# Branch gates loaded into more buffers, K's second half behind the first head, an earlier table of weight sums, and A22 ahead of s4 in a hybrid RWKV / RG-LRU encoder block

## The chip, the cores and the metric

The kernel runs on one core of one Trainium2 chip. The metric is the device time of one execution in microseconds (us). The engines of the core are TensorE (PE in the profile, with its weight loads PEld), VectorE (DVE), ScalarE (ACT), GpSimd (POOL) and SyncE (SP). SP issues most of the loads, POOL and ACT some; all data moves through the core's 16 DMA engines.

## The reference, cut to what matters

One encoder block over 512 positions of width 1024, float32 throughout. Two sequence mixers, an RWKV-7 recurrence (`y_a`) and a gated linear recurrence (`y_b`), are merged by sigmoid gates; then come cross-attention into 256 memory rows with 4 heads, a gated feed-forward net of width 2816 and a last RMS norm.

```python
h = rms_norm(x, norm_mix_g)
proj = h @ w_in + b_in
y_a = rwkv7_branch(proj[..., :cb0], ...) @ w_branch_a
y_b = rglru_branch(proj[..., cb0:cb1], proj[..., cb1:cb2], ...) @ w_branch_b
merged = sigmoid(proj[..., cb2:cg1]) * y_a + sigmoid(proj[..., cg1:]) * y_b
x = x + merged @ w_mix_out
x = x + cross_attention(rms_norm(x, norm_x_g), rms_norm(mem, norm_mem_g), w_cq, w_ckv, w_co)
x = x + conv_ffn(rms_norm(x, norm_ffn_g), w_ffn_in, ffn_conv_w, ffn_conv_b, w_ffn_out)
return rms_norm(x, norm_final_g)

def cross_attention(h, m, w_q, w_kv, w_o):    # q, k, v reshaped to 4 heads of 256
    ...
    sc = einsum('bqhd,bkhd->bhqk', q, k) * 256 ** -0.5
    o = einsum('bhqk,bkhd->bqhd', softmax(sc), v)
    return o @ w_o
def conv_ffn(h, w_in, conv_w, conv_b, w_out):
    u = h @ w_in
    gate = causal_dwconv(u[..., :D_FF], conv_w, conv_b)
    return (gelu(gate) * u[..., D_FF:]) @ w_out
```

## The kernel before

A tensor of activations lies in SBUF as blocks of 128 features by 512 positions. A float32 product of one 128-block of weights with one block of activations is three matmuls (`mm3`): each factor is split into a rounded high part and the low rest, and high·high, high·low and low·high are summed in PSUM. The weights are streamed from HBM in tiles of 128x1024, eight units of 128x128 each (`stream`, tag `wr`, 4 buffers): SP loads the raw tile, ScalarE casts the high part (tag `wh`, 3 buffers), VectorE subtracts for the low part (tag `wl`, 3).

The program runs through these stages:

- the norm and the in-projection `inproj`, 38 blocks of 128 columns (`in_ps`). Blocks 22 to 37 are the branch gates: their sigmoids are stored to a DRAM tensor `dG`, since SBUF has no room for them. Blocks 14 to 17 (`px_gates`, `px_scan`) and 18 to 21 (`py_block`) belong to the second mixer; the chunks of the RWKV recurrence run between these products. `ga` and `gx` are tags of that part's tiles, with two buffers each; the tag `st` holds stores of gates and the tiles `ge`.
- w_branch_b: for each of the 8 output blocks m, a gate `gb` is loaded from `dG[8+m]`, the product lies in PSUM as `yb_ps`, and VectorE multiplies both into `mB`.
- w_branch_a: in the same way with a gate `gta` from `dG[m]`; VectorE multiplies `ya_ps` by it and adds `mB`, ScalarE casts the high part `mg` and VectorE subtracts for the low part. `mg` is what w_mix_out multiplies (`mix_ps`).
- cross-attention: K and V of the memory, computed at the program's start, are loaded from DRAM (`dK`, `dV`) in two halves each, through tiles of tag `kv`, and split into high and low parts (`K2`, `V2`). K's first half belongs to heads 0 and 1, its second to heads 2 and 3. `q_head(hd)` makes a head's q, `attend(hd, q2)` its scores (`sc_ps`), exponentials (`ex`), transposes (`prT`) and output. The loads `kv` are issued by ScalarE.
- w_co, then the feed-forward net. Its two large products are done by a scheme with seven products of half size in place of eight; some of them need sums of two quarters of the weights. POOL makes these sums by DMAs that accumulate in DRAM (`dS` for the first product, `dO` for the second).
- the output projection: the products A11, A12, s1, s2, s3, s4, A22, whose raw weights come by SP from `in_wfo` or from the sums `dOs`. They collect in PSUM tiles `X` and `YZ` (`ox_ps`, `oyz_ps`); `ffn_out` adds them into the residual `xr`, and `final` normalises and stores the output.

The order of the work on each engine is set by a scheduler at compile time, which simulates the program. POOL's DMAs for `dS` are tied to matmuls by hand: `sum_behind(ins, n)` issues the next n of them behind a product, and the table `NSUM` says how many go behind each block of the in-projection. Later products issue a fixed number each.

Of the kernel before, what the change touches and what calls it, by code (L numbers as in the profile page):

```python
# [9 lines left out]
F32 = mybir.dt.float32  # L10
F32R = mybir.dt.float32r
AF = mybir.ActivationFunctionType
ALU = mybir.AluOpType
# [4 lines left out]
P = 128  # L18
T = 512
D = 1024  # L20
# [11 lines left out]
IN_REST = [22, 23, 24, 25, 26, 27, 28, 29, 30, 31, 32, 33, 34, 35, 36, 37, 14, 15, 16, 17, 18, 19, 20, 21]  # L32
NEARLY = 3
NMID = 10
IN_ORDER = IN_RWKV + IN_REST


# [17 lines left out]
def hybrid_block_kernel(ctx: ExitStack, tc: tile.TileContext, xT_d, mT_d, pv_d, cst_d, win_d, wk_d, wv_d,  # L55
                        lup_d, gup_d, rga_d, rgx_d, wba_d, wbb_d, wmix_d, wq_d, wo_d, wfi_d, wfo_d, out_d):
    nc = tc.nc
    V, S, PE = nc.vector, nc.scalar, nc.tensor
# [15 lines left out]
    def rw_ps(name, pool=None, tag="rw", **kw):  # L74
        return (pool or prw).tile([P, T], F32, tag=tag, name=name, **kw)
# [193 lines left out]
    with tc.tile_pool(name="p0", bufs=1, reuse_waits="tile") as p0:  # L269
# [62 lines left out]
        st = stream(wv_d, "wv")  # L332
        for hf in range(2):
            pss = [(mm_ps if hf else rw_ps)(f"v_ps{hf}_{i}") for i in range(2)]
# [107 lines left out]
    MQ = KB // 2  # L442
# [46 lines left out]
    tp = tp_ctx.enter_context(tc.tile_pool(name="tp", bufs=1, reuse_waits="tile"))  # L489
# [19 lines left out]
    for i in range(2):  # L509
        with tc.issue_after(wdma[-1].ins):  # L510
# [5 lines left out]

    NSUM = {12: 1, 13: 1, 4: 1, 5: 1, 0: 1, 1: 1, 8: 1, 9: 1, 6: 2, 7: 2, 2: 2, 3: 2, 10: 2, 11: 2,
            22: 2, 23: 1, 27: 1, 28: 1, 29: 1, 31: 1, 32: 1, 33: 1, 34: 1, 35: 1, 36: 1,
            17: 3, 18: 4, 19: 4, 20: 4, 21: 4}

    def inproj(i):
        nonlocal last_in
# [160 lines left out]
    with tc.tile_pool(name="pz", bufs=1, reuse_waits="tile") as pz:  # L683
# [9 lines left out]
        for s in range(30, -1, -1):  # L693
            n = 31 - s
# [249 lines left out]
            V.tensor_tensor(yb2[:, 1, b, :], yb, yb2[:, 0, b, :].bitcast(F32), ALU.subtract)  # L944
    ub = Units(wbb_d, "wbb")
    for m in range(KB):
        gb = tp.tile([P, T], F32, tag="st", name=f"gb{m}", bufs=2)
        nc.sync.dma_start(gb, dG[8 + m])
        psb = mm_ps(f"yb_ps{m}")
        dense(psb, ub, lambda kb: (yb2[:, 0, kb, :], yb2[:, 1, kb, :]), 4)  # L950
        V.tensor_tensor(mB[:, m, :], psb, gb, ALU.mult)
# [6 lines left out]
    pm = pm_ctx.enter_context(tc.tile_pool(name="pm", bufs=2, reuse_waits="tile"))  # L958
    ua = Units(wba_d, "wba")
    for m in range(KB):  # L960
        ga = pm.tile([P, T], F32, tag="ga", name=f"gta{m}")
        nc.sync.dma_start(ga, dG[m])
        psa = mm_ps(f"ya_ps{m}")
        dense(psa, ua, lambda kb: (ya2[:, 0, kb, :], ya2[:, 1, kb, :]), 4)
        V.tensor_tensor(ga, psa, ga, ALU.mult)
        V.tensor_tensor(ga, ga, mB[:, m, :], ALU.add)
        S.copy(mg2[:, 0, m, :], ga)
        V.tensor_tensor(mg2[:, 1, m, :], ga, mg2[:, 0, m, :].bitcast(F32), ALU.subtract)
# [46 lines left out]
    pk = pk_ctx.enter_context(tc.tile_pool(name="pk", bufs=1, reuse_waits="tile"))  # L1015
    K2 = pk.tile([P, 2, KB, NMEM], F32R, name="K2")
    V2 = pk.tile([P, 2, 2, D], F32R, name="V2")
    for i, what in ((0, "K"), (0, "V"), (1, "V"), (1, "K")):
        kv = pk.tile([P, D], F32, tag="kv", name=f"kv{what}{i}", bufs=2)
        if what == "K":  # L1020
            ks = slice(4 * i, 4 * i + 4)
            hi, lo = K2[:, 0, ks], K2[:, 1, ks]
            kv = kv.rearrange("p (m n) -> p m n", n=NMEM)
            nc.scalar.dma_start(kv, dK[ks].rearrange("m p n -> p m n"))
        else:
            hi, lo = V2[:, 0, i], V2[:, 1, i]
            nc.scalar.dma_start(kv, dV[i])
        S.copy(hi, kv)
        V.tensor_tensor(lo, kv, hi.bitcast(F32), ALU.subtract)

    uq = Units(wq_d, "wq")

    def q_head(hd, nsum=2):
        q2 = pk.tile([P, 2, 2, T], F32R, tag="q2", name=f"q2_{hd}", bufs=2)
        for i in range(2):
            ps = mm_ps(f"q_ps{hd}_{i}")
            dense(ps, uq, lambda kb: (hx[:, 0, kb, :], hx[:, 1, kb, :]), KB, nsum + i * (nsum > 0))
            S.copy(q2[:, 0, i, :], ps)
            V.tensor_tensor(q2[:, 1, i, :], ps, q2[:, 0, i, :].bitcast(F32), ALU.subtract)
        return q2  # L1040
# [35 lines left out]
    for hd in range(4):  # L1076
        attend(hd, q2)
        if hd < 3:
            q2 = q_head(hd + 1)

    pk_ctx.close()

# [5 lines left out]
    H = T // 2  # L1088
# [164 lines left out]
    def out_weights():  # L1253

        flat = []
        for n in ("A11", "A12", "s1", "s2", "s3", "s4", "A22"):
            for m, k in out_order:
                if n[0] == "A":
                    p, i = out_units(m, int(n[1]), int(n[2]))[k]
                    flat.append((p, wfo_d[p], i))  # L1260
                else:
                    flat.append(((n, m), dO["s2" if n == "s4" else n, m], k))
        for g in range(0, len(flat), 8):
            units = flat[g:g + 8]
            n = len(units) * P
            with tc.high_priority():
                raw = wp.tile([P, 1024], F32, tag="wr", name=f"wfo_r{g // 8}", bufs=4)
                k = 0
                while k < len(units):
                    key, src, i = units[k]  # L1270
                    e = k
                    while e < len(units) and units[e][0] == key and units[e][2] == i + e - k:
                        e += 1
                    nc.sync.dma_start(raw[:, k * P:e * P], src[:, i * P:(i + e - k) * P])
                    k = e
                hi = wp.tile([P, 1024], F32R, tag="wh", name=f"wfo_h{g // 8}")
                lo = wp.tile([P, 1024], F32R, tag="wl", name=f"wfo_l{g // 8}")
                S.copy(hi[:, :n], raw[:, :n])  # L1278
                V.tensor_tensor(lo[:, :n], raw[:, :n], hi[:, :n].bitcast(F32), ALU.subtract)  # L1279
            for k in range(len(units)):  # L1280
                yield hi[:, k * P:(k + 1) * P], lo[:, k * P:(k + 1) * P]
# [3 lines left out]
    def out_product(n, i, out, start, done, nsum=0):  # L1285

        for m, k in out_order:
            wh, wl = next(uf)
            g = gsets[i][k // 8][:, k % 8]
            ins = mm3(out[m], wh, wl, g[:, 0, :], g[:, 1, :], start and k == 0, k == HB - 1,  # L1290
                      skip_group_check=not start)
            if m * HB + k < nsum:
                sum_behind(ins)
            if k == HB - 1:
                done(m)
# [10 lines left out]
    YZ = [pf.tile([P, T], F32, tag="yz", name=f"oyz_ps{m}", bufs=4) for m in range(MQ)]  # L1306
    cols = (slice(0, H), slice(H, T))
    sn1, sn5 = ([pc.tile([P, T], F32, tag="sn", name=f"{n}_{i}", bufs=3) for i in range(2)] for n in ("o1", "o5"))
    sn6 = pc.tile([P, T], F32, tag="sn", name="o6_0", bufs=3)
    p1, p5 = ([t[:, c] for t in ts for c in cols] for ts in (sn1, sn5))  # L1310
    p6 = [sn6[:, c] for c in cols]
    p6 += [pc.tile([P, H], F32, tag="p5", name=f"o6_{m}", bufs=3) for m in (2, 3)]

    def ffn_out(src, snap, sign, m, ts, first=False, last=False):

        n = ts.stop - ts.start
        if snap is not None:
            t1 = pc.tile([P, T], F32, tag="s", name=f"t1_{m}_{ts.start}")
            V.tensor_tensor(t1[:, :n], src, snap, ALU.add)
            src = t1[:, :n]  # L1320
        V.tensor_tensor(xr[:, m, ts], xr[:, m, ts], src, sign)
        sq = sso[:, ts] if first else pc.tile([P, T], F32, tag="ac", name=f"t2_{m}_{ts.start}")[:, :n]
        S.activation(sq, xr[:, m, ts], AF.Square)
        S.activation(xr[:, m, ts], xr[:, m, ts], AF.Identity, scale=par("nfin", m))
        if not first and not last:
            V.tensor_tensor(sso[:, ts], sso[:, ts], sq, ALU.add)
        return sq

    def final(ts, sq, nb):
        n = ts.stop - ts.start  # L1330
        pss = rw_ps(f"rs_ps{ts.start}", pf, "yz", bufs=4)
        PE.matmul(pss[:, :n], ones, sso[:, ts], start=True, stop=False)
        PE.matmul(pss[:, :n], ones, sq, start=False, stop=True)
        rsqrt(ro[:, ts], pss[:, :n], 1.0 / D, eps[:, 0:1], load=False)
        for m in range(0, KB, nb):
            ms = slice(m, m + nb)
            V.tensor_tensor(xr[:, ms, ts], xr[:, ms, ts], ro[:, ts].unsqueeze(1).to_broadcast([P, nb, n]), ALU.mult)
            nc.sync.dma_start(out_d[:, ms, ts], xr[:, ms, ts])

    def c12(m):  # L1340
        sq = ffn_out(YZ[m][:, H:T], p6[m], ALU.add, m, cols[1], last=m == MQ - 1)
        if m == MQ - 1:
            final(cols[1], sq, 2)

    def c21(m):
        if m < MQ - 1:
            ffn_out(X[m], None, ALU.subtract, MQ + m, cols[0])
        else:
            for o in (0, P):
                ts = slice(o, o + P)  # L1350
                final(ts, ffn_out(X[m][:, ts], None, ALU.subtract, MQ + m, ts, last=True), 4)

    prepare(1, lambda ks: g2(ks, 1))
    prepare(2, lambda ks: g1(ks, 1))
# [7 lines left out]
    prepare(1, lambda ks: g2(ks, 2))  # L1362
    out_product("s1", 2, [t[:, H:T] for t in YZ], True, lambda m: S.copy(p5[m], YZ[m][:, H:T]))
    prepare(2, lambda ks: g1(ks, 2))
    out_product("s2", 0, X, False, lambda m: S.copy(p6[m], X[m]))
    for put in out_sums(("s4",)):
        tc.keep_in_program_order(put())
    for k in K4:
        ks = slice(k, min(k + 4, HB))
        V.scalar_tensor_tensor(g1(ks, 1), g1(ks, 1), -1.0, g2(ks, 1), ALU.mult, ALU.subtract)  # L1370
        split_g(0, lambda ks: g1(ks, 1), k)
    out_product("s3", 2, X, False, lambda m: ffn_out(X[m], p5[m], ALU.subtract, MQ + m, cols[1], first=m == 0))
    out_product("s4", 1, [t[:, H:T] for t in YZ], False, c12)
    out_product("A22", 0, X, False, c21)


# [75 lines left out]
```

## Time and profile before

| | |
|---|---|
| time, 3 runs | 908.43 us median (905.87 to 909.82) |
| profiled execution | 911.28 us, span 909.5 us, granted clock 0.998 |
| TensorE busy | 886.1 us (97%), 6186 matmul records |
| VectorE, ScalarE, POOL busy | 684.8, 515.8, 131.2 us |
| DMA | 201.37 MB, mean 221 GB/s |

All times of the profile are from one execution and count from the span's start. A line of the timeline reads: start in us, duration in us, engine, source line, operation, output tile and input tiles, shape, how many were put together; in brackets how long the engine was idle before it and what ended that idle time. An engine with a "q" at its end is the engine's queue at issuing a DMA. "L948" is line 948 of the kernel before; the numbers behind tile names in the lists of order below are the compiler's.

### The profile page before, as it was taken

Reading aid. Unit: us, or ns where it says so; the run is one execution under the profiler, and the core shown is the slowest. Engines: PE = TensorE matmul, PEld = TensorE weight load, DVE = VectorE, ACT = ScalarE, POOL = GpSimd, SP = SyncE. Lnnn points to the kernel's source line nnn. Section 1 sums busy time; section 2 is a strip of 40 time slices with the busy share of each in tenths; the row PEclk is TensorE's granted clock in tenths of the full one; section 3 lists DMA queues with packets and bytes.
Section 4 is the critical chain, followed back from the end, with each engine's and each line's share of the span. In section 5 each row is a group of like instructions: output and inputs, shape, how many; then the busy total and the mean of one; then the engine's idle time right before and its main releaser. Section 6 shows DMA issues by size and latency. Waiting matters only on the chain.

```text
span 909.5 us, 15907 instructions
## 1 busy us (share of the span) xinstructions
PE 886.1 (97%) x6186; PEld 769.3 (85%) x6186; DVE 684.8 (75%) x1100; ACT 515.8 (57%) x787; POOL 131.2 (14%) x161
## 2 busy tenths in 40 slices
PE   6999999999999999989989999999999999999996
PEld 6888878888877777768867778999999999999996
DVE  7884698768957686576566568889888888999674
ACT  6674676643347675134454356766655556757563
POOL 0102222021001122001012111111111111202100
PEclk9999999999999999999999999999999999999999
DMA  8879799677876289968887958899989998988963
GB/s 273 279 269 222 191 234 226 201 200 215 264 175 161 41 176 239 261 189 229 220 215 164 214 124 184 243 273 275 271 240 301 268 284 252 245 274 207 273 193 92
DMA packets 97642, 201.37 MB, mean 221 GB/s; under 512 B 19424, under 2 KB 30816, under 8 KB 97504
## 3 DMA queue, kind: packets, MB, share of 16 engines
q1 hardware_dynamic: 63584, 118.97, 40.0%
q0 software_dynamic: 25504, 67.38, 36.4%
q10 hardware_dynamic: 8480, 14.02, 4.5%
q8 instruction: 48, 0.79, 0.3%
q14 instruction: 26, 0.21, 0.1%
HBM read 188.54 MB, written 78.12 MB: 293 GB/s over the span
## 4 chain that ended last, share of the span: by engine, by line
PE 86%; DMA 7%; DVE 5%; ACT 1%; issue 1%; SPq 0%; DVEq 0%; ACTq 0%
PE in_ps L162 8%; PE in_ps L161 8%; PE in_ps L163 7%; PE fx_ps L162 5%; PE fx_ps L161 5%; PE fx_ps L163 5%; PE fyz_ps L162 3%; PE fyz_ps L163 3%; PE fyz_ps L161 3%; DMA gb<-dG 2%; PE ox_ps L163 2%; PE ox_ps L161 2%; PE ox_ps L162 2%; PE co_ps L161 2%; PE co_ps L163 2%; PE co_ps L162 2%
## 5 line engine op out<-in xcount | busy, mean ns | idle before, releaser
L127 ACT CAST wfi_h<-wfi_r 128x1024 fp32r<-128x1024 f32 x77 | 81.0, 1052 | 81.0 <-PE fyz_ps L162 28.4
L162 PE MATMUL in_ps<-hT,win_h 128*128 128x512 f32 x304 | 121.6, 402 | 0.0
L161 PE MATMUL in_ps<-hT,win_h 128*128 128x512 f32 x304 | 121.5, 401 | 0.1
L163 PE MATMUL in_ps<-hT,win_l 128*128 128x512 f32 x304 | 121.6, 401 | 0.0
L128 DVE TENSOR_TENSOR wfi_l<-wfi_r,wfi_h 128x1024 fp32r<-128x1024 f32 x77 | 94.1, 1222 | 23.0 <-ACT wfi_h L127 22.9
L427 POOL DMA_DIRECT2D dS<-in_wfi x66 | 66.5, 1028 | 267.8 <-PE in_ps L161 134.1
L116 DVE TENSOR_TENSOR win_l<-win_r,win_h 128x1024 fp32r<-128x1024 f32 x38 | 46.3, 1222 | 30.8 <-ACT win_h L115 30.1
L161 PEld LDWEIGHTS in_ps<-hT,win_h 128*128 128x128 f32 x304 | 57.0, 188 | 14.6 <-DVE pr L531 0.6
L162 PEld LDWEIGHTS in_ps<-hT,win_h 128*128 128x128 f32 x304 | 57.0, 188 | 14.5 <-issue 0.7
L163 PEld LDWEIGHTS in_ps<-hT,win_l 128*128 128x128 f32 x304 | 57.0, 188 | 14.2 <-issue 0.7
L463 POOL DMA_DIRECT2D dOs<-in_wfo x54 | 39.9, 789 | 188.4 <-PE fyz_ps L161 48.2
L115 ACT CAST win_h<-win_r 128x1024 fp32r<-128x1024 f32 x38 | 39.8, 1048 | 43.1 <-PE in_ps L162 40.4
L1279 DVE TENSOR_TENSOR wfo_l<-wfo_r,wfo_h 128x1024 fp32r<-128x1024 f32 (+1 forms) x39 | 47.1, 1209 | 16.2 <-ACT wfo_h L1278 14.6
L1278 ACT CAST wfo_h<-wfo_r 128x1024 fp32r<-128x1024 f32 (+1 forms) x39 | 40.4, 1038 | 30.2 <-DMA wfo_r<-dOs 8.0
L163 PE MATMUL ox_ps<-go,wfo_l 128*128 128x256 f32 x176 | 49.5, 281 | 1.2 <-DVE wfo_l L1279 1.2
L162 PE MATMUL fx_ps<-hr,wfi_h 128*128 128x256 f32 x176 | 49.8, 283 | 0.0
L161 PE MATMUL ox_ps<-go,wfo_h 128*128 128x256 f32 x176 | 49.8, 283 | 0.0
L163 PE MATMUL fx_ps<-hr,wfi_l 128*128 128x256 f32 x176 | 49.8, 283 | 0.0
L162 PE MATMUL fx_ps<-hq,wfi_h 128*128 128x256 f32 x176 | 49.4, 281 | 0.0
L162 PE MATMUL fyz_ps<-hq,wfi_h 128*128 128x256 f32 x176 | 49.4, 281 | 0.0
L161 PE MATMUL fx_ps<-hr,wfi_h 128*128 128x256 f32 x176 | 49.4, 280 | 0.0
L162 PE MATMUL ox_ps<-go,wfo_h 128*128 128x256 f32 x176 | 49.3, 280 | 0.0
(419 smaller groups left out, 2713.4 us busy)
## 6 DMA issues: line engine op xcount, KB each, us to landing
dS<-in_wfi POOLq DMA_DIRECT2D x66, 512.0 KB, 7.9
wfi_r<-dS SPq DMA_DIRECT2D x44, 512.0 KB, 6.3
win_r<-in_win SPq DMA_DIRECT2D x38, 512.0 KB, 5.6
wfi_r<-in_wfi SPq DMA_DIRECT2D x33, 512.0 KB, 5.9
dS<-dS POOLq DMA_DIRECT2D x22, 512.0 KB, 5.3
dOs<-in_wfo POOLq DMA_DIRECT2D x12, 512.0 KB, 7.1
wv_r<-in_wv SPq DMA_DIRECT2D x8, 512.0 KB, 4.9
dG<-gs ACTq DMA_DIRECT2D x16, 256.0 KB, 5.2
```

What stands on the lines that cost most here:

```text
L115: S.copy(hi[:, o:o + n], raw[:, o:o + n])
L116: V.tensor_tensor(lo[:, o:o + n], raw[:, o:o + n], hi[:, o:o + n].bitcast(F32), ALU.subtract)
L127: S.copy(hi, raw)
L128: V.tensor_tensor(lo, raw, hi.bitcast(F32), ALU.subtract)
L161: first = PE.matmul(ps, lh, rh, start=start, stop=False, **kw)
L162: PE.matmul(ps, lh, rl, start=False, stop=False, **kw)
L163: PE.matmul(ps, ll, rh, start=False, stop=stop, **kw)
L427: return lambda: nc.gpsimd.dma_start(s(out), src, **kw)
L463: yield lambda k=k, w=w, src=src: nc.gpsimd.dma_start(dO[n, m][:, k * P:(k + w) * P], src, **kw)
L1278: S.copy(hi[:, :n], raw[:, :n])
L1279: V.tensor_tensor(lo[:, :n], raw[:, :n], hi[:, :n].bitcast(F32), ALU.subtract)
```

## The change

Four edits.

1. The gates `gb` rotate through the tags ga, gx and st with two buffers each, six in place of two. `gta` has five buffers in place of two.
2. `NSUM` issues its sums behind other blocks: behind 17, 18 and 19 one more each, behind 20 and 21 fewer, behind 37 one. Together 18 where it was 19.
3. The tag kv has three buffers in place of two. K's first half and both halves of V are loaded ahead of head 0; K's second half is loaded after head 0's `attend` and head 1's q.
4. In the output projection, A22 and its weights come ahead of s4. What s2 put into `X` is added into `xr` at once by VectorE, where ScalarE made a copy that was added later. The last product is now s4, and its last block is normalised in two pieces of 128 positions, which A22's was before.

```diff
+KVB = 3
...
-            17: 3, 18: 4, 19: 4, 20: 4, 21: 4}
+            37: 1, 17: 4, 18: 5, 19: 5, 20: 2, 21: 1}
...
     for m in range(KB):
-        gb = tp.tile([P, T], F32, tag="st", name=f"gb{m}", bufs=2)
+        gb = tp.tile([P, T], F32, tag=("ga", "gx", "st")[m % 3], name=f"gb{m}", bufs=2)
         nc.sync.dma_start(gb, dG[8 + m])
...
-        ga = pm.tile([P, T], F32, tag="ga", name=f"gta{m}")
+        ga = pm.tile([P, T], F32, tag="ga", name=f"gta{m}", bufs=5)
...
-    for i, what in ((0, "K"), (0, "V"), (1, "V"), (1, "K")):
-        kv = pk.tile([P, D], F32, tag="kv", name=f"kv{what}{i}", bufs=2)
+
+    def load_kv(what, i):
+        kv = pk.tile([P, D], F32, tag="kv", name=f"kv{what}{i}", bufs=KVB)
...
+    load_kv("K", 0)
+    for i in range(2):
+        load_kv("V", i)
...
         attend(hd, q2)
         if hd < 3:
             q2 = q_head(hd + 1)
+        if hd == 0:
+            load_kv("K", 1)
...
-        for n in ("A11", "A12", "s1", "s2", "s3", "s4", "A22"):
+        for n in ("A11", "A12", "s1", "s2", "s3", "A22", "s4"):
...
-    def final(ts, sq, nb):
+    def final(ts, sq, nb, tag):
...
+    def c21(m):
+        sq = ffn_out(X[m], None, ALU.subtract, MQ + m, cols[0], last=m == MQ - 1)
+        if m == MQ - 1:
+            final(cols[0], sq, 2, "x")
+
     def c12(m):
-        sq = ffn_out(YZ[m][:, H:T], p6[m], ALU.add, m, cols[1], last=m == MQ - 1)
-        if m == MQ - 1:
-            final(cols[1], sq, 2)
-
-    def c21(m):
         if m < MQ - 1:
-            ffn_out(X[m], None, ALU.subtract, MQ + m, cols[0])
+            ffn_out(YZ[m][:, H:T], None, ALU.add, m, cols[1])
         else:
-            for o in (0, P):
+            for o in (H, H + P):
                 ts = slice(o, o + P)
-                final(ts, ffn_out(X[m][:, ts], None, ALU.subtract, MQ + m, ts, last=True), 4)
+                final(ts, ffn_out(YZ[m][:, ts], None, ALU.add, m, ts, last=True), 4, "yz")
...
-    out_product("s2", 0, X, False, lambda m: S.copy(p6[m], X[m]))
+    out_product("s2", 0, X, False,
+                lambda m: V.tensor_tensor(xr[:, m, cols[1]], xr[:, m, cols[1]], X[m], ALU.add))
...
+    out_product("A22", 0, X, False, c21)
     out_product("s4", 1, [t[:, H:T] for t in YZ], False, c12)
-    out_product("A22", 0, X, False, c21)
```

SP's queue at the loads for w_branch_b and w_branch_a (`wbb_r`, `wba_r` are raw weight tiles, `gb` the gates), before:

```order
L103 DMA wbb_r2_3633<-in_wbb 128x1024
L103 DMA wbb_r3_3671<-in_wbb 128x1024
L103 DMA wba_r0_3715<-in_wba 128x1024
L103 DMA wba_r1_3759<-in_wba 128x1024
L948 DMA gb0_3554<-dG_712 128x512
L103 DMA wba_r2_3803<-in_wba 128x1024
L948 DMA gb1_3576<-dG_712 128x512
L948 DMA gb2_3592<-dG_712 128x512
L948 DMA gb3_3614<-dG_712 128x512
```

The same place now:

```order
L104 DMA wbb_r2_3632<-in_wbb 128x1024
L949 DMA gb1_3575<-dG_712 128x512
L949 DMA gb0_3553<-dG_712 128x512
L949 DMA gb4_3629<-dG_712 128x512
L949 DMA gb3_3613<-dG_712 128x512
L104 DMA wbb_r3_3670<-in_wbb 128x1024
L104 DMA wba_r0_3714<-in_wba 128x1024
L104 DMA wba_r1_3758<-in_wba 128x1024
L949 DMA gb2_3591<-dG_712 128x512
L104 DMA wba_r2_3802<-in_wba 128x1024
L949 DMA gb5_3651<-dG_712 128x512
```

Four gates moved ahead of the last tile of w_branch_b and the first two of w_branch_a; gates 2 and 5 to 7 follow before the last tile of w_branch_a.

ScalarE's queue from the first cast of K2 to the first exponentials of head 0 (`kv` are the raw halves, `q_ps` products of q, `wq_h` high parts of q's weights), before:

```order
L1028 CAST K2_4240<-kvK0_4242 128x1024
L1028 CAST V2_4241<-kvV0_4246 128x1024
L1038 CAST q2_0_4258<-q_ps0_0_4259 128x512
L1027 DMA kvV1_4250<-dV_88 128x1024
L115 CAST wq_h4_4579<-wq_r4_4577 128x1024
L1024 DMA kvK1_4254<-dK_87 128x4x256
L1028 CAST V2_4241<-kvV1_4250 128x1024
L1038 CAST q2_0_4258<-q_ps0_1_4292 128x512
L1028 CAST K2_4240<-kvK1_4254 128x1024
L115 CAST wq_h5_4614<-wq_r5_4612 128x1024
L1038 CAST q2_1_4414<-q_ps1_0_4415 128x512
L1057 ACTIVATE ex0_0_4338,smst0_0_4335<-sc_ps0_0_4328,smst0_0_4335,rxc_4216 128x256
```

The same place now:

```order
L1029 DMA kvV1_4249<-dV_88 128x1024
L116 CAST wq_h4_4578<-wq_r4_4576 128x1024
L1043 CAST q2_0_4253<-q_ps0_0_4254 128x512
L1043 CAST q2_0_4253<-q_ps0_1_4287 128x512
L1030 CAST V2_4240<-kvV1_4249 128x1024
L1026 DMA kvK1_4481<-dK_87 128x4x256
L1062 ACTIVATE ex0_0_4333,smst0_0_4330<-sc_ps0_0_4323,smst0_0_4330,rxc_4215 128x256
L1062 ACTIVATE ex0_1_4349,smst0_1_4346<-sc_ps0_1_4339,smst0_1_4346,rxc_4215 128x256
L116 CAST wq_h5_4613<-wq_r5_4611 128x1024
L1030 CAST K2_4239<-kvK1_4481 128x1024
L1062 ACTIVATE ex0_2_4365,smst0_2_4362<-sc_ps0_2_4355,smst0_2_4362,rxc_4215 128x256
```

The load of K's second half and its cast moved: the load stands behind the cast of V's second half, the cast behind two exponentials. TensorE's matmuls are the same in number; their order differs in the attention, where scores, transposes and q interleave otherwise, and in the last two products.

More of the change, by code (lines that the diff above doesn't have):

```diff
@@ L1308, in hybrid_block_kernel @@
     sn1, sn5 = ([pc.tile([P, T], F32, tag="sn", name=f"{n}_{i}", bufs=3) for i in range(2)] for n in ("o1", "o5"))
-    sn6 = pc.tile([P, T], F32, tag="sn", name="o6_0", bufs=3)
     p1, p5 = ([t[:, c] for t in ts for c in cols] for ts in (sn1, sn5))
-    p6 = [sn6[:, c] for c in cols]
-    p6 += [pc.tile([P, H], F32, tag="p5", name=f"o6_{m}", bufs=3) for m in (2, 3)]
     def ffn_out(src, snap, sign, m, ts, first=False, last=False):
@@ L1327, in ffn_out @@
         return sq
-    def final(ts, sq, nb):
+    def final(ts, sq, nb, tag):
         n = ts.stop - ts.start
-        pss = rw_ps(f"rs_ps{ts.start}", pf, "yz", bufs=4)
+        pss = rw_ps(f"rs_ps{ts.start}", pf, tag, bufs=4)
         PE.matmul(pss[:, :n], ones, sso[:, ts], start=True, stop=False)
```

## The prediction

> **What bounds the kernel now.** I read the engine totals first, then the chain of work that ended last, then TensorE's waits by releaser, then stretches around the three places that the change touches.
>
> ```profile
> span 909.5 us, 15907 instructions
> PE 886.1 (97%) x6186; PEld 769.3 (85%) x6186; DVE 684.8 (75%) x1100; ACT 515.8 (57%) x787; POOL 131.2 (14%) x161
> ...
> PE 86%; DMA 7%; DVE 5%; ACT 1%; issue 1%; SPq 0%; DVEq 0%; ACTq 0%
> ```
> TensorE is busy 97% of the span. The change removes no matmul, so only 909.5 − 886.1 = 23.4 us can be won, and most of that is the start and the end.
>
> ```profile
> PE k_ps L161 <- ACT m L288: 6.5, 1, 6.5
> PE sc_ps L1050 <- ACT ex L1057: 2.6, 1, 2.6
> PE mix_ps L161 <- ACT mg L967: 1.3, 1, 1.3
> PE ya_ps L161 <- DVE mB L951: 1.3, 2, 0.7
> PE ox_ps L163 <- DVE wfo_l L1279: 1.2, 2, 0.8
> ```
> In each row stand the waiting engine and product, the releaser, us in total, times, and the longest. The 6.5 us of k_ps are the program's start. The others are the places that the change can reach. The same in stretches (width, then busy us of PE, PEld, DVE, ACT and POOL with their counts, granted clock, share of the 16 DMA engines, GB/s):
>
> ```profile
> 335.00:350.00 15.00, 15.00 (x67) 12.13 (x66) 9.14 (x13) 10.37 (x16) 3.86 (x5) 1.00 1.03 230
> 350.00:380.00 30.00, 28.27 (x117) 21.34 (x117) 17.24 (x27) 10.73 (x15) 3.73 (x4) 1.00 0.97 272
> 380.00:405.00 25.00, 23.38 (x100) 18.08 (x98) 19.58 (x27) 8.16 (x11) 0.71 (x1) 1.00 0.65 192
> 830.00:850.00 20.00, 19.24 (x162) 18.87 (x161) 13.41 (x13) 10.38 (x14) 5.71 (x7) 1.00 1.07 254
> ```
> 350–380 and 380–405 are w_branch_b and w_branch_a, 830–850 the output products. The granted clock is 1.00 throughout.
>
> **A, the gates' loads.** VectorE multiplies each block of w_branch_b by a gate gb that SP loads into one of two buffers, and each load waits until a buffer is free.
>
> ```profile
> 344.93 0.50 SPq L948 DMA_DIRECT2D gb<-dG  x1
> 350.52 9.52 SPq L948 DMA_DIRECT2D gb<-dG  x3
> 371.03 3.98 SPq L948 DMA_DIRECT2D gb<-dG  x2
> ...
> 370.31 0.69 DVE L951 TENSOR_TENSOR mB<-yb_ps,gb 128x512 f32<-128x512 f32 x1 [3.03 <-DMA gb<-dG]
> 377.67 0.69 DVE L951 TENSOR_TENSOR mB<-yb_ps,gb 128x512 f32<-128x512 f32 x1 [1.87 <-DMA gb<-dG]
> ...
>   DMA gb<-dG: 9.8, 6
> ...
> DMA to landing us min/median/max: 4.8/6.7/9.3
> ```
> The load that is issued when mB at 370.31 ends lands behind the last products of yb: VectorE idles 9.8 us on these loads, the PSUM banks stay full, and TensorE waits:
>
> ```profile
> 373.50 0.39 PE L162 MATMUL yb_ps<-yb,wbb_h 128*128 128x512 f32 x1
> 373.73 0.40 PE L163 MATMUL yb_ps<-yb,wbb_l 128*128 128x512 f32 x1
> 374.81 0.47 PE L161 MATMUL ya_ps<-ya,wba_h 128*128 128x512 f32 x1 [0.68 <-DVE mB L951]
> ...
> 402.57 0.40 PE L163 MATMUL mix_ps<-mg,wmix_l 128*128 128x512 f32 x1
> 404.31 0.73 PE L161 MATMUL mix_ps<-mg,wmix_h 128*128 128x512 f32 x2 [1.34 <-ACT mg L967]
> 404.89 0.40 PE L162 MATMUL mix_ps<-mg,wmix_h 128*128 128x512 f32 x1
> 405.97 0.50 PE L162 MATMUL mix_ps<-mg,wmix_h 128*128 128x512 f32 x1 [0.69 <-DVE mg L968]
> ```
> Matmuls of this shape start 0.23 us apart (373.50 to 373.73). A gap therefore costs its distance in starts less 0.23 for each matmul: 374.81 − 373.73 − 0.23 = 0.85; the mix pair 404.31 − 402.57 − 0.23 = 1.51 and 405.97 − 404.89 − 0.23 = 0.85. By the stretches, busy falls short by 1.73 in 350–380 and by 1.62 in 380–405. Added up gap by gap in the same way over 370 to 406, small ones too, TensorE loses 5.1 us. With six gb buffers, four of the eight loads go out as soon as the RWKV scans free ga and gx, before wbb_r3, and the other four stand ahead of wba_r3. The scans end some 20 us ahead of the first old load:
>
> ```profile
> 324.09 1.22 DVE L905 TENSOR_TENSOR_SCAN YB<-ga,xb 128x512 f32<-128x512 f32 x1
> ```
> So gates 0, 1, 3, 4 can land by about 325.3 + 9.3 = 335. gta with five buffers goes out as soon as the tiles under it are free. The mix pair is late because VectorE, which ran behind its waits on gb, is late with mg (the releasers in brackets). Without the 9.8 us it is early by more than the 2.36 us of that pair. I take 4.6 of the 5.1: 0.5 stays for the step from ya's last block through L965 to L968, which is a serial chain of VectorE and ScalarE that no buffer shortens. Bounds: 0 (loads late all the same) and −5.1.
>
> Behind the earlier gb loads on SP's queue stand wbb_r3 and wba_r0. These are covered: TensorE has 75.00 of 75 us busy in 260–335 and 15.00 of 15 in 335–350, and loses nothing there.
>
> **B, K's second half.** In the old order ScalarE's queue casts K1 before q of head 1 and before the first exponentials, and K1's load gets a buffer only once K0 is cast:
>
> ```profile
> 458.81 0.38 ACTq L1024 DMA_DIRECT2D kvK<-dK  x1
> 460.99 1.05 ACT L1028 CAST V<-kvV 128x1024 fp32r<-128x1024 f32 x1 [1.78 <-DMA kvV<-dV]
> 466.42 1.05 ACT L1028 CAST K<-kvK 128x1024 fp32r<-128x1024 f32 x1 [3.90 <-DMA kvK<-dK]
> 472.68 0.56 ACT L1057 ACTIVATE ex<-sc_ps,smst,rxc 128x256 f32<-128x256 f32 x1 [0.67 <-DVE smst L1055]
> ...
> 468.00 0.39 PE L161 MATMUL q_ps<-hx,wq_h 128*128 128x512 f32 x1
> 471.01 0.39 PE L1050 MATMUL sc_ps<-K,q 128*128 128x256 f32 x1 [2.62 <-ACT ex L1057]
> ```
> ScalarE stands 3.90 us for K1 while the scores of head 0 already wait for their exponentials. TensorE then stops for 471.01 − 468.00 − 0.23 = 2.78 us. In the new order the cast of K1 stands behind two exponentials, so these run as soon as VectorE has their sums. K1 is read first by head 2. Its load now goes out behind V1's cast, which ended at 460.99 + 1.05 ≈ 462.0 and has one 0.6 us evacuation of q more ahead of it now: about 463. The old K1 took 466.42 − 458.81 = 7.6 us, so it lands near 471, between the second and third exponential (472.68). What is late next is that third exponential, by at most about 1 us, and TensorE has q of heads 1 and 2 to fill it. I take −2.4; bounds −2.8, and +2 if K1 lands some 5 us later than the old one and holds the queue with its 3.9 us again, longer than the q products last.
>
> **C, the sums.** POOL issues the same sums in the same order. By the table, blocks 17 to 21 and 37 allow 4, 5, 5, 2, 1 and 1 of them in place of 3, 4, 4, 4, 4 and 0: 18 for 19, and earlier.
>
> ```profile
> dS<-in_wfi POOLq DMA_DIRECT2D x66, 512.0 KB, 7.9
> ...
> 357.99 0.71 POOL L427 DMA_DIRECT2D dS<-dS  x1 [10.59 <-DMA dS<-in_wfi]
> 399.31 0.71 POOL L427 DMA_DIRECT2D dS<-dS  x1 [34.31 <-PE mix_ps L161]
> ...
> 260.00:335.00 75.00, 75.00 (x1159) 55.95 (x1158) 51.25 (x98) 50.89 (x89) 10.35 (x11) 1.00 0.55 120
> ```
> The DMA share is 1.03 and 0.97 in 335–380 but 0.55 before, so moving sums forward moves bytes from a full stretch into a half-empty one. One sum less is up to 3 loads of 512 KB, at 272 GB/s 5.8 us of that stretch's 30. That helps A's loads and is in its number; by itself I take 0, bounds ±1. All later sums come one slot later. POOL waits 34.31 us for such a slot, so it is held by the table and not by the DMAs. The cover is FFN's own stretch, 575–800, where TensorE loses nothing:
>
> ```profile
> 575.00:800.00 225.00, 224.98 (x1892) 224.46 (x1890) 199.13 (x268) 140.61 (x202) 37.36 (x52) 1.00 0.93 268
> ```
>
> **D, A22 ahead of s4.** s4's product gets later, so its sums have the whole of A22's product as slack; four ScalarE copies go, and the additions that VectorE did in s4's evacuation stand at the end of s2. The gaps that exist are elsewhere:
>
> ```profile
> 843.95 2.20 ACT L1278 CAST wfo_h<-wfo_r 128x1024 fp32r<-128x1024 f32 x2 [4.45 <-DMA wfo_r<-dOs]
> 844.36 0.81 POOL L463 DMA_DIRECT2D dOs<-in_wfo  x1 [2.11 <-DMA wfo_r<-dOs]
> ```
> ScalarE stands 4.45 us for weights whose load is on its way, and that is what the 1.2 us of ox_ps on wfo_l in the waits come from, while DMA is at 1.07 with s4's own sums. Those sums follow s2's loads in time, before and after, so they still collide with the same loads. Since ScalarE idles there, its missing copies free nothing. The end has the same shape as before: one half in 256 columns, one in two pieces of 128, the last of both on VectorE, ScalarE and a DMA. I take 0; bounds ±1.2, the 1.2 us that TensorE waits for wfo_l being the most there is to win, and as much to lose where VectorE's four additions stand ahead of a weight's low part.
>
> **The sum.** −4.6 − 2.4 + 0 + 0 = −7.0. The profiled execution took 911.28 us, so it would become 904.3. It is 2.85 above the median of the runs, 908.43. If half of that excess is the same waits on DMAs, the median wins 7.0 − 1.4 = 5.6: 908.43 − 5.6 = 902.8. That half is an estimate, between none (901.4) and all (904.3). What a measurement here can tell from no change is 0.5%, 4.5 us, so the border of faster is 903.9.
>
> **Rivals.** R1, the wait moves: the 16 DMA engines are full in 335–380, so loads issued earlier finish little earlier, or wba and wmix come later by what gates take. Against it speaks the 0.55 of 260–335, into which half the gates move; for it, that gb took up to 9.3 us where SP was not in its way. A then gives 0 to −2 and B −1 to −2.4, together −1 to −4.4, of which the median shows 5.6/7.0: 904.9 to 907.6, about 906. The Trainium skill, "DMA: Bandwidth & Descriptors", section "Issuing engines are not separate DMA queues", says that all issuers share the same 16 DMA engines and interleave; read as a rule on this place it gives R1's time, and the shares of 1.03 and 0.97 agree that they can be full. Chance 0.27.
>
> R2, K1 keeps the stall: it lands late as in B's upper bound but less so, and B gives 0 while A holds: 908.43 − 4.6 × 5.6/7.0 = 904.7. Chance 0.10.
>
> R3, slower: the sums pulled into blocks 18 and 19, 3 × 512 KB each, at the 230 GB/s of 335–350 are 6.8 us of DMA each; two of them, with the early gates ahead of wbb_r3 and wba_r0, could hold w_branch_b's weights past 350. It decides once weights come over 12 us late: 13.6 − 7 gives +6.6, about 915. Against it, nothing of TensorE waits there now. Chance 0.05.
>
> **Chances.** The forecast 0.58, R1 0.27, R2 0.10, R3 0.05. The range 898.8 to 908.2 takes A and B at their full bounds and C and D together at −1.7 below (908.43 − 5.1 − 2.8 − 1.7), and all of R1 and R2 above, with 0.6 for D's loss; R3 is left out. Faster by over 0.5%: 0.57; within: 0.38; slower: 0.05.
>
> **What would show it.** After: VectorE's idle on gb under 2 us; no wait of ya_ps on mB and of mix_ps on mg of more than 0.5; in the first head, the first two exponentials before K1's cast and no 2.6 us of sc_ps on ex; waits of ox_ps on wfo_l still near 1.2. I am wrong if landing times of gb rise over 10 us, if a new wait of ya_ps or mix_ps on weights shows, or if the end after the last product grows.

## The result, and the profile after

The changed kernel takes 901.75 us against 908.5 us of the kernel before on the same chip (medians of nine runs each; before, they lie between 905.87 and 916.71): a ratio of 0.9913, 95% interval 0.9886 to 0.9939. Eight of the nine runs of the changed kernel lie between 900.65 and 901.96, and the ninth, a disturbed one of 2428.0 us, is left out of the ratio. The forecast was 902.8.

The page of the changed kernel, and its chain of work:

```profile
span 900.2 us, 15903 instructions
PE 882.2 (98%) x6186; PEld 768.9 (85%) x6186; DVE 683.2 (76%) x1100; ACT 514.2 (57%) x783; POOL 131.4 (15%) x161
...
PE 88%; DMA 5%; DVE 5%; ACT 1%; issue 1%; SPq 0%; DVEq 0%; ACTq 0%
```

TensorE's waits by releaser; the rows on mB, mg and ex that stood there before are gone:

```profile
PE k_ps L162 <- ACT m L289: 6.4, 1, 6.4
PE k_ps L164 <- DVE wk_l L117: 1.3, 2, 0.8
PE ox_ps L164 <- DVE wfo_l L1286: 0.8, 1, 0.8
...
PE ox_ps L162 <- ACT wfo_h L1285: 0.2, 1, 0.2
```

The stretches of w_branch_b, w_branch_a and w_mix_out (columns as before: width, busy PE, PEld, DVE, ACT, POOL, clock, DMA share, GB/s):

```profile
335.00:350.00 15.00, 15.00 (x67) 12.11 (x65) 8.89 (x12) 10.38 (x16) 3.17 (x4) 1.00 0.87 216
350.00:380.00 30.00, 29.59 (x128) 23.50 (x127) 21.75 (x33) 12.25 (x17) 2.87 (x3) 1.00 0.87 227
380.00:405.00 25.00, 25.00 (x109) 20.09 (x108) 20.02 (x28) 9.82 (x14) 1.43 (x2) 1.00 0.54 164
```

TensorE is busy 29.59 and 25.00 us where it had 28.27 and 23.38, and the DMA share has fallen from 1.03 and 0.97 to 0.87. SP's queue at the gates, what ended VectorE's idle time before mB, the landing times of gb, and TensorE at the two seams:

```profile
320.76 5.19 SPq L949 DMA_DIRECT2D gb<-dG  x4
345.18 0.35 SPq L949 DMA_DIRECT2D gb<-dG  x1
...
  PE yb_ps L164: 6.1, 4
...
DMA to landing us min/median/max: 3.1/6.8/8.1
...
373.42 0.39 PE L164 MATMUL yb_ps<-yb,wbb_l 128*128 128x512 f32 x1
373.65 0.40 PE L162 MATMUL ya_ps<-ya,wba_h 128*128 128x512 f32 x1
...
395.82 0.39 PE L164 MATMUL ya_ps<-ya,wba_l 128*128 128x512 f32 x1
396.05 0.40 PE L162 MATMUL mix_ps<-mg,wmix_h 128*128 128x512 f32 x1
```

The first four gates are issued from 320.76 on. A gate still takes 6.8 us at the median, but VectorE now waits for products only, and both seams run on at the matmul's pitch of 0.23 us. ScalarE in the first head:

```profile
454.59 0.38 ACTq L1026 DMA_DIRECT2D kvK<-dK  x1
...
458.34 0.56 ACT L1062 ACTIVATE ex<-sc_ps,smst,rxc 128x256 f32<-128x256 f32 x1 [2.44 <-DVE smst L1060]
458.90 0.56 ACT L1062 ACTIVATE ex<-sc_ps,smst,rxc 128x256 f32<-128x256 f32 x1
...
461.31 1.05 ACT L1030 CAST K<-kvK 128x1024 fp32r<-128x1024 f32 x1 [0.31 <-DMA kvK<-dK]
```

K's second half lands in 461.31 − 454.59 = 6.7 us, two exponentials are out ahead of it, and ScalarE stands 0.31 us in place of 3.90.

Set against each other by the start of TensorE's first and last matmul of each product, the two profiled executions (911.28 and 901.96, 9.32 apart) differ by +0.25 up to w_branch_b, −5.46 from there to the first q, −3.25 in the attention, −0.35 in the feed-forward input and −0.55 in the output products. The medians are only 6.75 apart: the execution of before that was profiled was longer than most.

### The profile page after: what moved, and what is told of

Same layout as the page of the kernel before. It is cut to its first block, busy times and chain, and to the rows that moved or that the text cites. A ratio compares the mean times of both kernels' runs of the same rounds, so it can differ in the third digit from the quotient of the medians.

```text
span 900.2 us, 15903 instructions
## 1 busy us (share of the span) xinstructions
PE 882.2 (98%) x6186; PEld 768.9 (85%) x6186; DVE 683.2 (76%) x1100; ACT 514.2 (57%) x783; POOL 131.4 (15%) x161
## 4 chain that ended last, share of the span: by engine, by line
PE 88%; DMA 5%; DVE 5%; ACT 1%; issue 1%; SPq 0%; DVEq 0%; ACTq 0%
PE in_ps L163 8%; PE in_ps L162 8%; PE in_ps L164 8%; PE fx_ps L162 4%; PE fx_ps L163 4%; PE fx_ps L164 4%; PE fyz_ps L162 3%; PE fyz_ps L163 3%; PE fyz_ps L164 3%; DMA wfo_r<-dOs 2%; PE co_ps L162 2%; PE q_ps L163 2%; PE mix_ps L164 2%; PE mix_ps L163 2%; PE q_ps L164 2%; PE mix_ps L162 2%
```

## Experiments

The kernel before moves by some tenths of a per cent from call to call, so each kernel stands as a ratio to the runs of before on its own chip, with the 95% interval.

| kernel | us | before | ratio (95%) | branches | attention | output |
|---|---|---|---|---|---|---|
| before, first profile | 911.28 | | | 96.3 | 70.5 | 113.0 |
| before, second profile | 915.87 | | | 100.0 | 73.3 | 112.1 |
| edit 1 alone | 902.21 | 909.88 | 0.9905 (0.9885 to 0.9926) | 90.8 | 67.7 | 111.0 |
| gb's six buffers alone | 902.95 | 910.77 | 0.9913 (0.9884 to 0.9943) | 93.5 | 67.8 | 110.8 |
| gta's five buffers alone | 907.75 | 910.77 | 0.9964 (0.9945 to 0.9983) | 97.8 | 67.6 | 112.8 |
| edit 2 alone | 902.57 | 910.77 | 0.9908 (0.9883 to 0.9932) | 91.0 | 68.3 | 110.9 |
| edit 3 alone | 911.28 | 909.88 | 1.0009 (0.9987 to 1.0030) | 95.0 | 67.5 | 113.5 |
| edit 4 alone | 911.13 | 909.88 | 1.0007 (0.9987 to 1.0028) | 95.1 | 67.7 | 112.8 |
| all but edit 3 | 901.58 | 910.77 | 0.9900 (0.9874 to 0.9925) | 90.8 | 67.5 | 111.1 |
| all four | 901.75 | 908.50 | 0.9913 (0.9886 to 0.9939) | 90.8 | 67.3 | 112.5 |
| copy ahead of K, with edit 1 | 904.28 | 908.68 | 0.9947 (0.9925 to 0.9969) | 90.8 | 69.7 | 112.3 |
| sums later | 912.42 | 908.68 | 1.0039 (1.0017 to 1.0060) | 103.7 | 67.7 | 111.0 |
| sums later, with edit 1 | 908.33 | 908.68 | 0.9986 (0.9961 to 1.0011) | 96.5 | 67.7 | 112.4 |
| all four, s4's sums behind s3 | 905.53 | 908.68 | 0.9968 (0.9950 to 0.9986) | 90.8 | 67.2 | 115.3 |

The last three columns are from the one profiled execution of each kernel, as differences between starts of matmuls: from the first of `yb_ps` to the first of `q_ps`, from there to the first of w_co (`co_ps`), and from the first of `ox_ps` to the start of the last row of `rs_ps`, which puts four matmuls together. Each holds the same matmuls in all kernels, so that 90.8, about 67.5 and about 111 are these stages with next to nothing lost.

**The kernel before once more.** No edit; a second profile.

> The kernel before, profiled a second time. Theory: the first profile was of an execution with more waiting than the median, by 911.28 - 908.43 = 2.85 us, and half of this is in the same waits on gate loads; then this execution is near 908.4 and TensorE loses between 350 and 406 some 3.5 to 4 us in place of 5.1. Rival: the excess lies elsewhere (start, output), and the loss between 350 and 406 is 5 us again.

It took 915.87 us, more than the first. The branches take 100.0 us, 9.2 more than the 90.8 without waits, where the first profile lost 5.5. The attention takes 73.3, 5.8 more than 67.5, where the first lost 3.0, and the wait for K is there again:

```profile
PE sc_ps L1050 <- ACT ex L1057: 3.0, 1, 3.0
```

The theory's numbers failed, for this execution was not near the median but worse still. What it shows is that the loss in these two stretches changes from execution to execution. In the profiles of edit 3 alone and of edit 4 alone, in which the gates' loads are those of before, the branches lose 4.2 and 4.3.

**Edit 1 alone.**

```diff
-        gb = tp.tile([P, T], F32, tag="st", name=f"gb{m}", bufs=2)
+        gb = tp.tile([P, T], F32, tag=("ga", "gx", "st")[m % 3], name=f"gb{m}", bufs=2)
-        ga = pm.tile([P, T], F32, tag="ga", name=f"gta{m}")
+        ga = pm.tile([P, T], F32, tag="ga", name=f"gta{m}", bufs=5)
```

> Before with the buffers of gb and gta alone (edit 1). Theory: this is the larger part; the waits of ya_ps on mB and mix_ps on mg go, time 4 to 5 us less than before, 903.5 to 904.5. Rival (the DMA engines are full in 335 to 380, and it was the moved sums that made room): 1 to 2 us less only, with waits of ya_ps on mB left.

902.21, 7.7 us less than before: more than the theory's 4 to 5, and all that the whole change brings. There is no gap on mB or mg. The DMA engines are nearly as full as before in this stretch, since the sums stand in their old place:

```profile
335.00:350.00 15.00, 14.73 (x64) 11.57 (x62) 9.76 (x15) 10.38 (x16) 3.72 (x4) 1.00 0.99 250
350.00:380.00 30.00, 29.86 (x128) 24.04 (x129) 21.54 (x32) 11.30 (x15) 3.73 (x4) 1.00 0.95 278
```

So the rival fell: the gain does not need the room that moved sums make. The first four gates go out from 319.50 on, ahead of the full stretch. But the wait of the first head is gone too, though K is loaded in the old order, and so are the waits in the output products. That asked for the next one.

**Edit 3 alone.**

```diff
+KVB = 3
-    for i, what in ((0, "K"), (0, "V"), (1, "V"), (1, "K")):
-        kv = pk.tile([P, D], F32, tag="kv", name=f"kv{what}{i}", bufs=2)
+    def load_kv(what, i):
+        kv = pk.tile([P, D], F32, tag="kv", name=f"kv{what}{i}", bufs=KVB)
...
+        if hd == 0:
+            load_kv("K", 1)
```

> Before with K's second half behind head 0 and three kv buffers alone (edit 3). Theory: the 2.62 us wait of sc_ps on ex goes, 2.5 to 3.2 us less than before, 905.2 to 906. Rival: in its old place behind a late w_branch_a the cast of K's second half holds ScalarE again and the gain is under 1 us.

Its profile has no wait on ex, as the theory says, but its time is that of before: 1.0009, and the interval excludes a gain over 1.2 us. What its profile does have is the wait behind the gates:

```profile
PE yb_ps L162 <- DVE mB L952: 2.3, 1, 2.3
```

**Edit 4 alone.** The diff is that of the change from `out_weights` on.

> Before with A22 ahead of s4 alone (edit 4). Theory: no change, within 1 us of before, and waits of ox_ps on wfo near 1.2 us. Rival: the four copies that ScalarE no longer makes, and the later need of s4's sums, give 1 us or more.

No change, 1.0007, as the theory says; the waits in the output products are 1.5 us in its profile (0.7 on wfo_h and 0.8 on wfo_l). Its code is that of before up to the output products, and yet it shows no wait on ex. K's second half on ScalarE's queue, and the copy `dS<-dS` that POOL issues next, in this kernel and then in the one with edit 1 alone:

```profile
457.97 0.38 ACTq L1024 DMA_DIRECT2D kvK<-dK  x1
462.75 1.05 ACT L1028 CAST K<-kvK 128x1024 fp32r<-128x1024 f32 x1 [0.21 <-DMA kvK<-dK]
...
459.12 0.71 POOL L427 DMA_DIRECT2D dS<-dS  x1 [17.47 <-PE q_ps L161]
```

```profile
451.80 0.38 ACTq L1024 DMA_DIRECT2D kvK<-dK  x1
456.60 1.05 ACT L1028 CAST K<-kvK 128x1024 fp32r<-128x1024 f32 x1 [0.76 <-DMA kvK<-dK]
...
452.89 0.71 POOL L427 DMA_DIRECT2D dS<-dS  x1 [17.47 <-PE q_ps L161]
```

And that copy in the kernel before, where K's load was issued at 458.81 and took 7.6 us:

```profile
459.35 0.71 POOL L427 DMA_DIRECT2D dS<-dS  x1 [17.48 <-PE q_ps L161]
```

K's load was issued 1.15 and 1.09 us ahead of the copy and took 4.8 us; in the kernel before it was 0.54 us ahead (0.53 in its second profile, 7.9 us). So it looks as if K loses to the copy when it is issued just ahead of it.

**The copy ahead of K.** On top of edit 1, the first sum of head 1's q is issued at the end of head 0's q. The scheduler also interleaved scores and q otherwise on TensorE; ScalarE's order from K's load to the exponentials stayed.

```diff
+                  0 if hd == 1 and i == 0 else nsum + i * (nsum > 0), {(0, 1): 6, (1, 0): 4}.get((hd, i)))
```

(The last argument names a weight unit behind which one sum is issued.)

> The kernel with the gates' buffers alone, K in the old order, and the sum that POOL issues about 1.1 us behind K1's load there pulled ahead to the end of head 0's q (behind the 7th of 8 weight units), so that it is issued some 0.5 to 1 us ahead of K1's load; the second sum of that product stays where it was. Theory (whether K1's load is issued well ahead of that sum's copy decides if it lands in 4.8 or in 7.6 us): K1 lands in 7 us or more, TensorE waits 2 to 3 us for ex again, time 904 to 905. Rival (the landing times vary by chance): K1 lands in about 4.8, no wait, time near 902.2.

POOL's copy, K's load and cast, and TensorE:

```profile
452.86 0.71 POOL L427 DMA_DIRECT2D dS<-dS  x1 [15.60 <-PE q_ps L161]
...
453.53 0.38 ACTq L1024 DMA_DIRECT2D kvK<-dK  x1
460.93 1.05 ACT L1028 CAST K<-kvK 128x1024 fp32r<-128x1024 f32 x1 [3.30 <-DMA kvK<-dK]
...
465.51 0.39 PE L1051 MATMUL sc_ps<-K,q 128*128 128x256 f32 x1 [1.76 <-ACT ex L1058]
```

With the copy 0.67 us ahead, K takes 7.4 us, ScalarE stands 3.30, TensorE waits again. The time is 904.28, ratio 0.9947 (0.9925 to 0.9969), against 0.9905 with edit 1 alone. The theory's landing time and time are met, the wait is a little under its 2 us. The two intervals just touch, but the profile agrees with the medians: the attention is 2.0 us longer than with edit 1 alone. The other six profiles with K in the old order fit. With POOL's next sum 0.82 to 1.20 us behind K's load, it took 4.1 to 4.7 us in five of them; with the sum 0.77 us behind, in edit 2 alone, it took 5.8. So the wait that edit 3 removes is real, and it hangs on this order of issue; but as edit 3 alone gains nothing, the median execution of before can hardly have it.

**All but edit 3.** The changed kernel with K's old order and two kv buffers.

> The changed kernel without edit 3: K in the old order, two kv buffers. Theory 1 (K's order is worth its 2.4 us whenever K's second half lands late): 2 us and more slower than the changed kernel, 903.8 or above beside its 901.75. Theory 2 (with the gates loaded early K lands in about 4.8 us as in the run with the gates alone, ScalarE does not stand): within 1 us of it, no sc_ps wait on ex over 1 us.

901.58, ratio 0.9900: the second theory. Beside edits 1 and 2, K's new order brings nothing that can be measured.

**gb alone, gta alone.** The two lines of edit 1, one each.

> Before with six buffers for gb alone, gta as before. Theory: the waits of yb_ps and ya_ps on mB go, and most of the pair of mix_ps on mg, since VectorE no longer starts w_branch_a late; 4 to 6 us less. Rival: gta's two buffers hold VectorE in w_branch_a just as long, 1 to 3 us less only, with ya_ps on gta and mix_ps on mg left.

> Before with five buffers for gta alone, gb as before. Theory: w_branch_b's waits stay (ya_ps or yb_ps on mB, 2 us), those in w_branch_a and mix_ps shrink by half; 1 to 3 us less. Rival: no change.

gb alone gives 7.8 us, more than expected, and no wait on mB. In its profile a pair of waits in w_mix_out stays, `mix_ps` on `mg` for 1.8 us at the longest. gta alone gives 3.0 in time, as expected, but not where it was expected: in its profile `yb_ps` on mB (2.2) remains, and `mix_ps` on mg is still 2.0, as long as the two waits of before together. gb carries the edit.

**Edit 2 alone.**

```diff
-            17: 3, 18: 4, 19: 4, 20: 4, 21: 4}
+            37: 1, 17: 4, 18: 5, 19: 5, 20: 2, 21: 1}
```

> Before with the new table of sums alone (edit 2). Theory: within 1 us of before; the waits on mB and mg stay. Rival (the loads of the gates are late for want of DMA room): 2 us and more less, and gb lands in under 6 us at the median where it took 6.7.

This was the surprise: 902.57, 8.2 us less, as much as edit 1, with two buffers for gb. The last of POOL's sums before w_mix_out, what ended VectorE's idle time before mB, gb's landing, and the stretch of w_branch_b:

```profile
353.52 1.14 POOL L427 DMA_DIRECT2D dS<-in_wfi  x1 [2.88 <-PE yb_ps L163]
...
  DMA gb<-dG: 4.0, 3
...
DMA to landing us min/median/max: 2.6/4.9/6.8
...
350.00:380.00 30.00, 29.60 (x128) 23.79 (x128) 21.43 (x32) 11.57 (x16) 1.78 (x2) 1.00 0.88 234
```

Between 350 and 390 POOL issues one DMA of the sums, at 353.52, where the kernel before issues four from 357.99 on. The DMA share of 350 to 380 falls from 0.97 to 0.88, gb lands in 4.9 us in place of 6.7, and no wait on mB is left. The rival was right.

**The sums later, without and with edit 1.** As many sums in all as before, moved to later blocks.

```diff
-            17: 3, 18: 4, 19: 4, 20: 4, 21: 4}
+            17: 2, 18: 3, 19: 4, 20: 5, 21: 5}
```

> Before with the table moved the other way: 2, 3, 4, 5, 5 sums behind blocks 17 to 21, as many in all, later by one or two each. Theory (sums that run beside w_branch_b take the DMA engines from the gates' loads): slower than before by 1 to 4 us, gb's median landing above 6.7 us, VectorE idle on gb over 9.8 us. Rival (only the sum left out at the end mattered): as before.

> The same late table with the gates' buffers of the change. Theory (early loads make the time independent of the sums): 901.5 to 903.5 as with the old table, no wait of ya_ps or yb_ps on mB. Rival: some of the waits come back, 905 or more.

Without edit 1 it takes 912.42, ratio 1.0039 (1.0017 to 1.0060): slower, and the place of the sums alone does it, since there are as many as before. Its profiled execution, of 916.34 us, is the longest of its twelve. Seven DMAs of the sums go out between 355 and 373. gb's rows:

```profile
  DMA gb<-dG: 17.0, 4
...
DMA to landing us min/median/max: 5.2/7.4/10.9
```

With edit 1 it takes 908.33, ratio 0.9986 (0.9961 to 1.0011), no better than the kernel before, though 4.1 us better than the late table without edit 1. The theory's time fell and its rival's held, but not its reason: gb is waited for no longer and there is no wait on mB; now it is gta, whose rows in this kernel are

```profile
  DMA gta<-dG: 6.4, 1
...
DMA to landing us min/median/max: 2.7/9.9/13.3
...
PE mix_ps L161 <- ACT mg L967: 2.0, 1, 2.0
```

Early gates shift the need, and the next loads in the same full stretch meet the sums.

**s4's sums behind s3.** The changed kernel with the nine sums for s4 issued behind the first twelve units of s3.

```diff
-    for put in out_sums(("s4",)):
-        tc.keep_in_program_order(put())
+    sums = out_sums(("s4",))
...
-    out_product("s3", 2, X, False, lambda m: ffn_out(X[m], p5[m], ALU.subtract, MQ + m, cols[1], first=m == 0))
+    out_product("s3", 2, X, False, lambda m: ffn_out(X[m], p5[m], ALU.subtract, MQ + m, cols[1], first=m == 0), 12)
```

> The changed kernel with s4's sums issued behind the first 12 units of product s3 in place of as soon as s2's loads are done. Theory: the transfers of these 9 sums leave the stretch in which the weights of s2 and s3 come late, waits of ox_ps on wfo_h and wfo_l (1.0 us in the changed kernel's profile) go, 0 to 1.5 us less than 901.75. Rival: s4's weights come late themselves and TensorE waits for wfo in front of s4.

905.53, ratio 0.9968 (0.9950 to 0.9986), a miss: the waits grew from 1.0 to 3.0 us. The rival was nearer, but it named the wrong product; the waits lie in A22, ahead of s4:

```profile
PE ox_ps L164 <- DVE wfo_l L1286: 1.5, 2, 0.8
PE ox_ps L162 <- ACT wfo_h L1285: 1.5, 2, 1.1
```

The raw weights `wfo_r` took up to 15.7 us to land, where the changed kernel's took up to 11.0: the sums collided with the loads for the next products. No kernel tried is clearly better than the changed one.

## Why the prediction was right, and where it was not

The time came within 1.1 us, and the forecast signs in the profile after all held: no wait on mB or mg, VectorE's idle time on gb gone, the first two exponentials ahead of K's cast, 1.0 us of `ox_ps` on wfo. That the total came so near is in part luck, for the runs size its terms otherwise: of the 5.6 us forecast for the median A stood for 3.7 and B for 1.9, and measured alone A brought 7.7, B nothing and C, put at nothing, 8.2.

- **A, the gates' loads, −4.6 (bounds 0 to −5.1).** Place and mechanism right: −5.46 in the profiled pair, and edit 1 alone has all of the gain (7.7 us on the medians, though not all of it in these seams). The step that was mis-sized is the outer bound: it took the 5.1 us of one execution as the most there is, and another lost 9.2. The first profile has none of the slow matmuls that follow some waits (last section). Beyond these seams, edit 1 alone also came without the waits in the first head and in the output; the first of these goes with K's load being issued further ahead of the copy, the second stays open (below).
- **B, K's second half, −2.4.** The profiled pair shows −3.25 and thus seems to confirm it, but edit 3 alone is 1.0009 and its removal 0.9900 beside 0.9913. The step that failed: the wait of 2.62 us was priced as if nearly every execution had it. Of the ten profiles with K in the old order, the copy experiment aside, two have it (2.6 and 3.0 us), one has 0.6 and seven have none. The two are both profiles of the unchanged kernel, in executions longer than its median; that the median does not have it follows from edit 3 alone, not from a profile. The copy experiment shows what it hangs on. The path was also read in part only. Not just ScalarE stood for K: VectorE, whose subtraction for K's low part comes ahead of its work on the scores, stood nearly as long, and the first exponential waited for VectorE (profile of before):

```profile
467.50 1.23 DVE L1029 TENSOR_TENSOR K<-kvK,K 128x1024 fp32r<-128x1024 f32 x1 [3.61 <-ACT K L1028]
470.30 0.56 ACT L1057 ACTIVATE ex<-sc_ps,smst,rxc 128x256 f32<-128x256 f32 x1 [1.40 <-DVE smst L1055]
```

- **C, the sums, 0 ± 1.** The step that failed most: "that helps A's loads and is in its number; by itself I take 0". By itself it is −8.2. The row was read rightly, shares of 1.03 and 0.97 against 0.55 earlier, and even the 5.8 us that one sum takes there; it was not drawn from it that this alone could clear the waits. Terms A and C are two cures of one cause, loads that land late in the full stretch of 335 to 380: A issues four gates ahead of it, C takes sums out of it. They do not add, for each alone already brings the branches to 90.8 and 91.0 us: 0.9905 and 0.9908 alone, 0.9913 with all four edits and 0.9900 without edit 3.
- **D, A22 ahead of s4, 0 ± 1.2.** Right: 1.0007.
- **The step from the profiled execution to the median.** −7.0 was cut to −5.6 since the execution shown was 2.85 us above the median. Right in kind: the pair differs by 9.32, the medians by 6.75.
- **R1 (the DMA engines are full).** It did not happen to this change, nor to edit 1 alone, where the shares were still 0.99 and 0.95: half the gates landed ahead of the full stretch. With three more sums in it, R1 came true: the late table with edit 1 gains 4.1 us over the late table without, not 7.7, and the wait moves on to gta. The rule that the prediction quoted for it, from the Trainium skill's "DMA: Bandwidth & Descriptors", section "Issuing engines are not separate DMA queues", agrees with the runs: where gb has two buffers, its loads, issued by SP, land the later the more sums POOL issues between 350 and 390 (at the median 4.9 us with one of them, 6.7 to 7.1 in five profiles with four, 7.4 with seven).

Left open: the output products take 110.8 to 111.1 us in five profiles and 112.1 to 113.5 in eight, across the edits and on both sides of edit 4. The eight have waits of `ox_ps` on wfo of 0.8 to 1.5 us and the five have none, but why the weights come late in some of them, no run shows.

## What to carry to other kernels

When a load is late in a stretch whose DMA share is near 1, look for the other transfers in that stretch first: taking three background sums out of it was worth as much here as tripling the buffers, and the buffers gave about half as much once three more sums ran there. Price a wait from more than one execution when it hangs on which of two transfers is issued first; both profiles of the kernel before showed some 3 us on K, and taking that wait away gained nothing at the median. Edits against one cause are to be summed as the larger of them, not added.

## What the runs showed that was not expected

Half a microsecond of issue order changes a landing time by more than half: the 512 KB of K's second half took 4.8 us when issued 1.09 and 1.15 us ahead of a DRAM copy of the same size, 7.6 and 7.9 us at 0.54 and 0.53 ahead, and 7.4 us at 0.67 behind.

A wait of TensorE can cost more than its own length. With edit 4 alone, TensorE starts again after 2.31 us of idle time, and a little later its matmuls come 0.43 us apart in place of 0.23, at a lower granted clock (the third column from the end of the stretches):

```profile
371.37 0.40 PE L163 MATMUL yb_ps<-yb,wbb_l 128*128 128x512 f32 x1
374.07 0.50 PE L161 MATMUL yb_ps<-yb,wbb_h 128*128 128x512 f32 x1 [2.31 <-DVE mB L951]
...
375.60 0.63 PE L161 MATMUL yb_ps<-yb,wbb_h 128*128 128x512 f32 x1
376.03 0.63 PE L162 MATMUL yb_ps<-yb,wbb_h 128*128 128x512 f32 x1
...
378.99 0.40 PE L163 MATMUL ya_ps<-ya,wba_l 128*128 128x512 f32 x1
...
370.00:380.00 10.00, 7.69 (x27) 5.78 (x26) 4.47 (x6) 1.04 (x1) 0.00 (x0) 0.83 0.81 248
380.00:390.00 10.00, 10.00 (x45) 8.03 (x44) 6.87 (x10) 2.74 (x4) 0.00 (x0) 1.00 0.70 248
```

The gap costs 374.07 − 371.37 − 0.23 = 2.47 us, and eight matmuls from 375.60 to 378.99 some 1.5 us more. Six of the fourteen profiles have such a stretch in the branches, among them the second one of before; there the granted clock is 0.51 from 475 to 480, behind the wait for K, and the 3.0 us of that wait go with 5.8 us lost in the attention. It does not follow every wait: not the 2.62 us in the first profile of before, nor 2.15 us with gta alone. What decides it, no run shows.

And the scatter goes with the waits: twenty-three runs of before in one call spread over 7.8 us (905.56 to 913.35), the eight runs of the changed kernel from 900.65 to 901.96 over 1.3.
